# Which of two sets of PSUM banks a group takes, and when the down projection's combinations are issued

## The chip, the core and the metric

The program runs on one core of one Trainium2 chip. The metric is device microseconds of one execution. In this text PE is TensorE's matmul, PEld its weight load, DVE is VectorE, ACT is ScalarE, POOL is GpSimd, and SP is SyncE, which issues most of the loads.

## The reference, cut to what matters

The program is one encoder block on 256 rows of width 2048: a mixer of four parts, cross attention, and a gated feed-forward network (SwiGLU) of inner width 5632, each with a norm and a residual. Everything is float32. The change lies in the feed-forward network:

```python
def swiglu(h, w_gate_up, w_down):
    gate, up = jnp.split(h @ w_gate_up, 2, axis=-1)
    return (jax.nn.silu(gate) * up) @ w_down
...
        x = x + swiglu(rms_norm(x, norm_g[l, 2]), w_gate_up[l], w_down[l])
    return rms_norm(x, final_norm_g)
```

## The kernel before, in words

**Matmuls.** A float32 product is made of three matmuls of 128 x 128 by 128 x 512: high part of the activations times high part of the weights, high times low, low times high (`part`, L433 to L435). The 256 rows are two blocks of 128, so that one 128 x 512 block of weights gives six matmuls. The weights come as slabs of 1 MB (16 blocks of 128 x 128) from one array `W`, in the order of their use, into three buffers `raw`. A slab is split in halves: ACT casts the high part `wh` (L135, L159) and DVE subtracts it to get the low part `wl` (L136, L160). The buffers of the halves come free when PE has used them.

**Slabs of two kinds.** In the feed-forward network most work goes by `paired_rows` (L452). A plan tells what each slab is. `N` is a plain slab: four inner indices k, two row blocks, 24 matmuls. `S` is a slab for one pair of inner indices by a scheme of seven products in place of eight (Strassen's, in Winograd's form): its weights are summed on DVE first (L157, and for the gate and up projection partly in the loads, tile `two`), its activations are combined on DVE (`combine`, L438: eight adds and subtracts on 128 or 256 columns, plus two casts on ACT), and it has 21 matmuls. Four of the seven products go into sums of their own, called 1, 5, 6 and 7 in the code; the others go into the plain results a0, a1, b0, b1 (a and b are the two column blocks of 512, 0 and 1 the two row blocks).

**Banks.** PSUM has eight banks of 128 x 512. Four belong to a pool that `gbank` draws from (tiles `pg`) and four to a pool of `bank` (tiles `pm`). Within `paired_rows`, `put` (L465) draws a bank when a name is first used: a0, a1, b0, b1 from `gbank`, the sums from `bank`. A pool gives its four banks in turn, and the first matmul into a bank waits until the last reader of the tile that held it is done.

**Gate and up projection** (`gate_up`, L1033). Eleven groups of 512 + 512 columns. The first runs without sums; the ten others follow the plan `GROUP = "NNSNSNSN"`, 5 x 24 + 3 x 21 = 183 matmuls each. After the last S of a group `mixed` (L1050) reads the sums: a copy of q1 on ACT (L1053), then DVE adds with q6, q7 and q5. `gated` (L1059) adds a0 and a1 to the gate and applies Silu on ACT, and after the last N `upped` (L1065) adds b0 and b1, multiplies, transposes (L543) and stores the hidden rows to memory by POOL (L545).

**Down projection** (`down`, L1124). Two passes of 22 slabs, by the plans

```python
PASSES = "NNNNNNSNNSNNSNNSNNSNNN", "NNSNSNSNSNSNSNNNNNNNNN"
```

The hidden rows come back turned by POOL (L550) and are split by ACT and DVE (L291, L283). The combinations of the five S of the first pass and the sixth of the second come from a generator, `combined` (L1137).

**What sets the order.** The program is written in one order, with generators (`Background`) stepped in between when an estimate of PE's progress says so (`poll`) or when something must be ready (`drain` steps one until it ends). From that text a scheduler makes an order for each engine, and it may move an instruction when it takes its bank or operand to be late. Where one group with sums follows another (j = 2 to 10 in `gate_up`), it lets the group before the change begin with ten matmuls into a0, and the first into a1 is the eleventh.

Of the kernel before, what the change touches and what calls it, by code (L numbers as in the profile page):

```python
# [27 lines left out]
DFF = 5632  # L28
# [16 lines left out]
GROUP = "NNSNSNSN"  # L45
# [159 lines left out]
class Background:  # L205
# [17 lines left out]
    def first(self, g):  # L223

        self.q.sort(key=lambda e: e[0] is not g)
# [29 lines left out]
class Block:  # L255
# [193 lines left out]
        for i, x in enumerate((v, w)):  # L449
            self.split2(z[:, i * R:i * R + R], z[:, 512 + i * R:512 + i * R + R], x)  # L450

    def paired_rows(self, w, cols, slots, sums, plan, mixed, first, ready=None, late=0, before=None):  # L452

        st, s, nk = self.st, len(sums), len(slots)
        rest = [k for k in range(nk) if not any(k in ks for ks, _ in sums)]
        steps = [(c, k) for c in range(2) for k in rest]  # L460
        todo, q = iter(sums), {}
        count = {"a0": len(rest) + s, "a1": len(rest) + s, "b0": len(rest) + s, "b1": len(rest)}
        left, total = {}, 0

        def put(name, hi, lo, wh, wl):  # L465
            if name not in q:
                q[name] = self.gbank() if name in count else self.bank()
                left[name] = count.get(name, s)
            new = left[name] == count.get(name, s)
            left[name] -= 1  # L470
            self.part(q[name][:, :], hi, lo, wh, wl, new, left[name] == 0)

        form = lambda t, r: (t[:, r * P:(r + 1) * P], t[:, R + r * P:R + (r + 1) * P])
        n = done = 0
        for i, kind in enumerate(plan):
            if before:
                before(i)
            if kind == "S":
                ks, z = next(todo)
                a = [form(slots[ks[0]], 0), form(slots[ks[1]], 0), form(slots[ks[1]], 1)]  # L480
                x1, s2, s3, x4 = ((z[:, i * P:i * P + P], z[:, 512 + i * P:512 + i * P + P]) for i in range(4))
                t = (("5", x1), ("7", s3))
                pairs = iter((("1", a[0]), ("b0", x4), ("a0", a[1]), *(t if st.n // 16 in SUMMED else t[::-1]), ("a1", a[2]), ("6", s2)))
                for parts in st.take_sums(w, ks, cols):
                    for wh, wl in parts:
                        name, (hi, lo) = next(pairs)
                        put(name, hi, lo, wh, wl)
                        self.bg.poll()
                done += 1
                if done == s:  # L490
                    mixed(*(q[i] for i in "1567"))
            else:
                for c, k in steps[n:n + 4]:
                    if ready:
                        ready(k)
                    wh, wl = st.take(w, k, cols[c], 4)
                    for r in range(2):
                        put("ab"[c] + str(r), *form(slots[k], r), wh, wl)
                        self.bg.poll()
                n += 4  # L500
            if first and done == s and n >= len(rest):
                first(q["a0"], q["a1"])
                first = None
        assert n == len(steps) - late and done == s
        return [q["b0"], q["b1"]], rest[len(rest) - late:]
# [527 lines left out]
    def gate_up(self, gp, f, z):  # L1033

        nc = self.nc
        box, g, stored = {}, {}, []

        def gate(ps):
            for r in range(2):
                g[r] = gp.tile([P, 512], F32, name=f"g{r}", tag=f"g{r}")  # L1040
                nc.scalar.activation(g[r], ps[r], AF.Silu, scale=box["col"][:, r:r + 1])

        def up(j, ps, h=None):
            h = h or [gp.tile([P, 512], F32, name="h", tag="h", bufs=2) for _ in range(2)]
            for r in range(2):
                self.stt(h[r], ps[r], box["col"][:, r:r + 1], g[r], ALU.mult, ALU.mult)
                self.store_turned(self.ff, 4 * j, r, g[r], h[r])
            stored.append(self.bg.now)

        def mixed(q1, q5, q6, q7):  # L1050

            g[0], g[1], h[0], h[1] = (gp.tile([P, 512], F32, name=n, tag=n, bufs=b) for n, b in (("g0", 1), ("g1", 1), ("h", 2), ("h", 2)))
            nc.scalar.copy(g[0], q1)  # L1053
            self.tt(h[0], g[0], q6, ALU.add)
            self.tt(g[1], h[0], q7, ALU.add)
            self.tt(h[0], q5, h[0], ALU.subtract)
            self.tt(h[1], q5, g[1], ALU.subtract)

        def gated(*ps):  # L1059

            for r in range(2):
                self.tt(g[r], g[r], ps[r], ALU.add)
                nc.scalar.activation(g[r], g[r], AF.Silu, scale=box["col"][:, r:r + 1])

        def upped(j, ps):  # L1065

            for r in range(2):
                self.tt(h[r], h[r], ps[r], ALU.add)
            up(j, h, h)

        h = {}

        def fetch(k0, k1, ahead, pause, wait=0):

            m = {}
            for k in range(k0, k1 + ahead):
                if k < k1:
                    while len(stored) <= k // 4:
                        yield
                    m[k] = self.tmp()  # L1080
                    self.load_turned(m[k], self.ff, k)
                if k >= k0 + ahead:
                    while wait and self.bg.now < stored[(k - ahead) // 4] + wait:
                        yield
                    mark = self.mark()
                    self.split(f[k - ahead], m.pop(k - ahead))
                    self.keep_place(mark)
                    self.have = k - ahead + 1
                    yield pause

        def norm():

            mark = self.mark()
            nc.scalar.activation(self.mg[:, 0:1], self.mg[:, 0:1], AF.Silu)
            self.keep_place(mark)
            yield 2.0
            self.row_norm(1, box)
            yield

        arrival = lambda: gp.tile([P, R], F32, name="ar", tag="ar", bufs=4)  # L1100
        last = self.bg.add(self.arrive(self.xf[1], 3, arrival, self.put3, FAR), go=True)
        col = self.bg.add(norm())

        def combined():
            for ks, z in sums:
                yield 3.0
                yield from self.combine(z, *(self.h3[k] for k in ks))

        sums = [((2 * i, 2 * i + 1), z[i]) for i in range(GROUP.count("S"))]
        comb = self.bg.add(combined())  # L1110
        ps = self.gemm_rows("w_gate_up", [0, DFF], self.h3,
                            parts=[(range(8), [0]), (range(8, 12), [0]), (range(12), [1]), (range(12, 16), [0]), (range(12, 16), [1])],
                            before=lambda n: n in (1, 3) and self.bg.drain(self.late if n == 1 else last))
        self.bg.drain(col)
        gate(ps[0])
        up(0, ps[1])
        early = self.bg.add(fetch(0, FT - 22, 3, 2.0, 15))
        self.bg.drain(comb)
        for j in range(1, DFF // 512):
            upped(j, self.paired_rows("w_gate_up", [j * 512, DFF + j * 512], self.h3, sums, GROUP, mixed, gated)[0])  # L1120
        self.bg.drain(early)
        self.fetch = self.bg.add(fetch(FT - 22, FT, 6, SOON))

    def down(self, f, sp):  # L1124
# [9 lines left out]
        sums = [((2 * i, 2 * i + 1), x) for i, x in enumerate(z)]  # L1134
        made, split = [], []
# [31 lines left out]
        def done(c, *ps):  # L1167

            for r, p in enumerate(ps):
                x = self.half(c, r)  # L1170
                self.tt(x, x, p, ALU.add)
                squares(x, c, r)
# [6 lines left out]
        for i, plan in enumerate(PASSES):  # L1179
            n = plan.count("S")  # L1180
            g = self.bg.add(combined(n))
            late = (0, LATE)[i]
            plan = plan[:22 - late // 4]

            def before(j):
                if j == plan.index("S"):
                    self.bg.drain(g)
                if late and j == len(plan) - 2:
                    st.extra = None

            ps, rest = self.paired_rows("w_down", [2 * i * 512, (2 * i + 1) * 512], f, sums[:n], plan,
                                        lambda *q: mixed(2 * i, *q), lambda *q: done(2 * i, *q), ready, late, before)
            if i == 0:
                done(1, *ps)
        return ss, ps, rest, split
# [681 lines left out]
```

## Time and profile before

| | |
|---|---|
| median of 3 runs | 1444.63 us (1441.95 to 1446.84) |
| the profiled execution's own time | 1443.87 us |
| its span | 1442.1 us |
| matmul and weight load pairs on PE | 6601 |
| gate and up projection, j = 2 to 10 | about 819 to 1198 us of the span |
| down projection, first pass | about 1198 to 1318 us |

The span runs from the program's first to its last instruction on the engines. Matmuls are pipelined: a 128 x 512 matmul shows a length of 0.39 us and the next one begins 0.227 us after it, so that PE is busy without a gap while it is fed. An idle stretch before an instruction stands in brackets behind it, with what ended it. A wait is put down to the instruction that came last.

### The profile page before, as it was taken

To read this page: it belongs to the slowest core of one execution; us is meant where nothing else is said; L and a number is where in the kernel's file an instruction comes from. 1 tells how busy PE (TensorE), PEld (TensorE's weight loads), DVE (VectorE), ACT (ScalarE), POOL (GpSimd) and SP (SyncE) were. 2 spreads that over 40 slices of the span, in tenths; PEclk is the share of its full clock that TensorE was granted. 3 is DMA by queue.
4 is the path that set the end of the run, shared out by engine and by line. 5 is a ranking of instruction groups with operands and counts; after the bars stand their busy time and mean duration, and the time that the engine had idled before them with its cause. 6 is when DMAs were issued, how large, how long until landed. Compare 5 with 4: busy or idle time off the path is not lost.

```text
span 1442.1 us, 18599 instructions
## 1 busy us (share of the span) xinstructions
PE 1426.6 (99%) x6601; PEld 1183.1 (82%) x6601; DVE 1125.6 (78%) x1681; ACT 807.5 (56%) x1160; POOL 234.8 (16%) x306
## 2 busy tenths in 40 slices
PE   9999999999999999999999999999999999999997
PEld 8888888888888888888888888888888878788886
DVE  6667868777977666676676888889888889978884
ACT  7556655446655555555555555555555556555553
POOL 0000100012312233530421112112211103000000
PEclk9999999999999999999999999999999999999999
DMA  9886564456667788864976998989999877645563
GB/s 357 296 287 242 204 216 152 170 180 220 204 204 222 240 260 266 270 207 153 295 238 206 281 304 272 284 266 279 280 290 294 263 229 266 200 180 193 216 221 130
DMA packets 73039, 343.80 MB, mean 238 GB/s; under 512 B 10958, under 2 KB 12655, under 8 KB 45169
## 3 DMA queue, kind: packets, MB, share of 16 engines
q1 hardware_dynamic: 54848, 288.98, 57.4%
q0 software_dynamic: 17664, 52.97, 15.4%
q8 instruction: 52, 0.85, 0.2%
q10 hardware_dynamic: 432, 0.66, 0.1%
q14 instruction: 43, 0.34, 0.1%
HBM read 322.12 MB, written 20.45 MB: 238 GB/s over the span
## 4 chain that ended last, share of the span: by engine, by line
PE 93%; DVE 3%; DMA 2%; ACT 1%; issue 0%; ACTq 0%; DVEq 0%
PE pg L433 25%; PE pg L435 25%; PE pg L434 25%; PE pg L381 4%; DMA raw<-in_W 2%; PE pm L434 2%; PE pm L433 2%; PE pm L435 2%; PE pg L382 2%; DVE wl L136 1%; PE pm L1330 1%; PE pm L1008 1%; ACT wh L135 1%; PE pm L979 1%; DVE wl L160 0%
## 5 line engine op out<-in xcount | busy, mean ns | idle before, releaser
L136 DVE TENSOR_TENSOR wl<-raw,wh 128x1024 fp32r<-128x1024 f32 (+1 forms) x421 | 504.6, 1212 | 175.4 <-ACT wh L135 172.1
L135 ACT CAST wh<-raw 128x1024 fp32r<-128x1024 f32 (+1 forms) x421 | 433.2, 1043 | 303.1 <-PE pg L435 216.0
L433 PE MATMUL pg<-wh,act 128*128 128x512 f32 (+1 forms) x1454 | 567.9, 391 | 3.4 <-DVE g L283 3.3
L434 PE MATMUL pg<-wl,act 128*128 128x512 f32 (+1 forms) x1454 | 566.5, 390 | 2.1 <-DVE wl L160 1.1
L435 PE MATMUL pg<-wh,act 128*128 128x512 f32 (+1 forms) x1454 | 566.1, 390 | 0.5 <-DVE act L283 0.5
L433 PEld LDWEIGHTS pg<-wh,act 128*128 128x128 f32 x1454 | 273.3, 188 | 63.5 <-DVE g L283 5.9
L434 PEld LDWEIGHTS pg<-wl,act 128*128 128x128 f32 x1454 | 273.3, 188 | 59.1 <-DVE wl L136 2.3
L435 PEld LDWEIGHTS pg<-wh,act 128*128 128x128 f32 x1454 | 273.1, 188 | 58.2 <-DVE act L283 1.1
L159 ACT CAST wh<-raw 128x1024 fp32r<-128x1024 f32 (+1 forms) x134 | 122.4, 918 | 143.9 <-PE pg L435 82.9
L160 DVE TENSOR_TENSOR wl<-raw,wh 128x1024 fp32r<-128x1024 f32 (+1 forms) x134 | 139.0, 1058 | 63.4 <-ACT wh L159 63.1
L381 PE MATMUL pg<-act,wh 128*128 128x512 f32 x256 | 90.5, 395 | 0.0
L382 PE MATMUL pg<-act,wl 128*128 128x256 f32 x256 | 71.8, 280 | 0.0
L102 POOL DMA_DIRECT2D two<-in_W x30 | 26.6, 886 | 243.6 <-DMA two<-in_W 138.3
L159 ACT CAST wh<-two 128x1024 fp32r<-128x1024 f32 x30 | 31.5, 1051 | 52.6 <-PE pg L435 43.6
L381 PEld LDWEIGHTS pg<-act,wh 128*128 128x128 f32 x256 | 48.1, 188 | 10.5
L157 DVE TENSOR_TENSOR raw<-raw 128x512 f32<-128x512 f32 x74 | 51.1, 690 | 1.7
L550 POOL DMA_DIRECT2D tmp<-hidden x44 | 38.8, 889 | 58.3 <-issue 22.1
L382 PEld LDWEIGHTS pg<-act,wl 128*128 128x128 f32 x256 | 48.2, 188 | 0.2
L160 DVE TENSOR_TENSOR wl<-two,wh 128x1024 fp32r<-128x1024 f32 x30 | 36.7, 1223 | 7.2 <-ACT wh L159 7.1
L545 POOL DMA_DIRECT2D hidden<-g x22 | 17.2, 788 | 143.3 <-DVE g L543 143.3
L434 PE MATMUL pg<-wl,f 128*128 128x512 f32 x94 | 36.6, 389 | 0.0
L435 PE MATMUL pg<-wh,f 128*128 128x512 f32 x94 | 36.6, 389 | 0.0
(362 smaller groups left out, 1678.0 us busy)
## 6 DMA issues: line engine op xcount, KB each, us to landing
raw<-in_W SPq DMA_DIRECT2D x216, 1024.0 KB, 5.6
raw<-in_W SPq DMA_DIRECT2D x30, 768.0 KB, 6.7
two<-in_W SPq DMA_DIRECT2D x60, 256.0 KB, 5.0
two<-in_W POOLq DMA_DIRECT2D x30, 512.0 KB, 9.2
raw<-in_W SPq DMA_DIRECT2D x11, 512.0 KB, 7.2
hidden<-g POOLq DMA_DIRECT2D x22, 256.0 KB, 3.7
tmp<-hidden POOLq DMA_DIRECT2D x44, 128.0 KB, 5.5
features<-tmp POOLq DMA_DIRECT2D x32, 128.0 KB, 5.0
```

Source lines behind the costliest of these rows:

```text
L102: nc.gpsimd.dma_start(t, W[:, 512:1536], accum_op=ALU.add)
L135: nc.scalar.copy(wh[:, a:b], r[:, a:b])
L136: nc.vector.tensor_tensor(out=wl[:, a:b], in0=r[:, a:b], in1=wh[:, a:b].bitcast(F32), op=ALU.subtract)
L157: nc.vector.tensor_tensor(out=out, in0=a, in1=b, op=ALU.add)
L159: nc.scalar.copy(wh, src)
L160: nc.vector.tensor_tensor(out=wl, in0=src, in1=wh.bitcast(F32), op=ALU.subtract)
L381: self.nc.tensor.matmul(p[:, :], wh, slot[:, :], start=start, stop=False)
L382: self.nc.tensor.matmul(p[:, 0:R], wl, slot[:, 0:R], start=False, stop=stop)
L433: self.nc.tensor.matmul(p, hi, wh, start=start, stop=False)
L434: self.nc.tensor.matmul(p, hi, wl, start=False, stop=False)
L435: self.nc.tensor.matmul(p, lo, wh, start=False, stop=stop)
L550: self.nc.gpsimd.dma_start(t.rearrange("p (g t) -> p g t", t=32), src)
```

## The change

Two things. In `paired_rows` a new argument `swap` lets the two pools trade places: with it a0, a1, b0 and b1 come from `bank` and the sums from `gbank`. It is set for every second group of the gate and up projection (j = 2, 4, 6, 8, 10) and for the second pass of the down projection. Also the four sums are drawn together when the first of them is used, in the order 1, 6, 7, 5. In the down projection the drain of the generator at the first S is gone: at each S it is stepped only until as many combinations are made as that S needs, and otherwise it goes on as a background generator.

```diff
-    def paired_rows(self, w, cols, slots, sums, plan, mixed, first, ready=None, late=0, before=None):
+    def paired_rows(self, w, cols, slots, sums, plan, mixed, first, ready=None, late=0, before=None, swap=False):
...
         def put(name, hi, lo, wh, wl):
             if name not in q:
-                q[name] = self.gbank() if name in count else self.bank()
-                left[name] = count.get(name, s)
+                for x in [name] if name in count else "1675":
+                    q[x] = (self.bank if (name in count) == swap else self.gbank)()
+                    left[x] = count.get(x, s)
...
         for j in range(1, DFF // 512):
-            upped(j, self.paired_rows("w_gate_up", [j * 512, DFF + j * 512], self.h3, sums, GROUP, mixed, gated)[0])
+            upped(j, self.paired_rows("w_gate_up", [j * 512, DFF + j * 512], self.h3, sums, GROUP, mixed, gated, swap=j % 2 == 0)[0])
...
             def before(j):
-                if j == plan.index("S"):
-                    self.bg.drain(g)
+                while plan[j] == "S" and len(made) <= plan[:j].count("S"):
+                    self.bg.step(next(e for e in self.bg.q if e[0] is g))
...
             ps, rest = self.paired_rows("w_down", [2 * i * 512, (2 * i + 1) * 512], f, sums[:n], plan,
-                                        lambda *q: mixed(2 * i, *q), lambda *q: done(2 * i, *q), ready, late, before)
+                                        lambda *q: mixed(2 * i, *q), lambda *q: done(2 * i, *q), ready, late, before, i == 1)
```

## The prediction

> **What bounds the kernel now.** I read the page first: how much of the span TensorE (PE) works.
>
> ```profile
> span 1442.1 us, 18599 instructions
> PE 1426.6 (99%) x6601; PEld 1183.1 (82%) x6601; DVE 1125.6 (78%) x1681; ACT 807.5 (56%) x1160; POOL 234.8 (16%) x306
> ```
>
> The profiled execution took 1443.87 us, 1.8 over its span. All sums below start from it; it is 0.76 under the median of the three runs, 1444.63 (1441.95 to 1446.84). PE idles 15.5 us in all, so a change that leaves the matmuls as they are can win only where PE stops. The waits of PE say at whom it stops (us in total, times, longest):
>
> ```profile
> PE pg L433 <- DVE g L283: 3.3, 5, 1.0
> PE pg L434 <- DVE wl L160: 1.1, 1, 1.1
> PE pm L587 <- DVE eps L588: 1.1, 1, 1.1
> PE pg L434 <- DVE wl L136: 1.0, 1, 1.0
> PE pg L435 <- DVE act L283: 0.5, 1, 0.5
> ```
>
> Apart from L587, at the program's start, these are the two places that the diff touches: five stops where a group of the gate and up projection begins, three in the first pass of the down projection. First one of the five, in PE's timeline (start, length, line):
>
> ```profile
> 944.81 0.39 PE L433 MATMUL pg<-wh,act 128*128 128x512 f32 x1
> ...
> 946.85 0.39 PE L433 MATMUL pg<-wh,act 128*128 128x512 f32 x1
> 947.99 0.50 PE L433 MATMUL pg<-wh,act 128*128 128x512 f32 x1 [0.75 <-DVE g L283]
> 948.32 0.39 PE L434 MATMUL pg<-wl,act 128*128 128x512 f32 x1
> ```
>
> Ten matmuls start between 944.81 and 946.85, so one takes 2.04 / 9 = 0.227. Across the stop the starts lie 1.14 apart (0.91 too many), and the next two 0.33 (0.11 too many): 0.75 of idle time cost 1.02, so a stop costs its idle time plus 0.27. VectorE (DVE) in the same stretch:
>
> ```profile
> 940.78 0.68 DVE L283 TENSOR_TENSOR h<-g,pm 128x512 f32<-128x512 f32 x1
> ...
> 946.11 1.23 DVE L136 TENSOR_TENSOR wl<-raw,wh 128x1024 fp32r<-128x1024 f32 x1 [1.12 <-ACT wh L135]
> 947.25 0.68 DVE L283 TENSOR_TENSOR g<-g,pg 128x512 f32<-128x512 f32 x1
> 947.85 1.28 DVE L283 TENSOR_TENSOR h<-h,pg 128x512 f32<-128x512 f32 x2
> ...
> 951.59 1.19 DVE L136 TENSOR_TENSOR wl<-raw,wh 128x1024 fp32r<-128x1024 f32 x1
> ```
>
> The add of 947.25 (`gated`, second row block) empties the bank that the eleventh matmul wants. It stands behind the weight split of 946.11, which waited 1.12 for a cast on ScalarE (ACT). What the cast waits for shows in the chain of waits of the group before (start, length, what), whose next links are the cast and the split:
>
> ```profile
> 894.83 7.57 DMA raw<-in_W
> ```
>
> A 1 MB load of 7.57, the cast, the split of 1.23, then the add: the bank comes late because its add queues behind a late load, not because DVE is short of time.
>
> **The change, part by part.** *The banks.* With the sets trading places at every group, a0 takes the bank that held q1 of the group before, and a1 that of q6 ("1675" is the order in which `mixed` reads them). The order of the changed program confirms it: a1's first matmul stands fourth instead of eleventh and waits for the add that reads q6. q1 is copied here:
>
> ```profile
> 935.80 0.58 ACT L1053 COPY g<-pm 128x512 f32<-128x512 f32 x1
> ```
>
> That ends at 936.38, 8.4 before the group's first matmul (944.81). The add of q6 (940.78) ends at 941.46, 4.0 before the fourth matmul (944.81 + 3 x 0.227 = 945.49). Both release far ahead of need, so the five stops go: 3.3 + 5 x 0.27 = **4.65**. The other way round, the four sums now take the banks of a0, a1, b0, b1. The last reader of those is the pair of adds at 947.85, done by 949.13; the first sum's matmul stands 48 matmuls into the group, at 944.81 + 48 x 0.227 = 955.7. Cover 6.6, cost nothing. No instruction is added and no shape changes; ACT, POOL and SP keep their order in this stage.
>
> What is late next: the split of 951.59, second half of the group's second slab, done at 952.78. Its matmul stands 37 in: 944.81 + 37 x 0.227 = 953.21. So 0.43 is left, and 0.18 at the longest stop (1.0, 0.25 more than this one). I cost it at nothing; its cover is thin, and a load longer by more than that turns into a stop there.
>
> *The combinations.* The three stops of the down projection, and DVE before them:
>
> ```profile
> 1234.13 0.39 PE L433 MATMUL pg<-wh,act 128*128 128x512 f32 x1
> 1235.65 0.50 PE L434 MATMUL pg<-wl,act 128*128 128x512 f32 x1 [1.12 <-DVE wl L160]
> ...
> 1238.06 0.51 PE L434 MATMUL pg<-wl,act 128*128 128x512 f32 x1 [0.97 <-DVE wl L136]
> ...
> 1242.04 0.73 PE L435 MATMUL pg<-wh,act 128*128 128x512 f32 x2 [0.51 <-DVE act L283]
> ```
>
> ```profile
> 1229.81 1.22 DVE L160 TENSOR_TENSOR wl<-raw,wh 128x1024 fp32r<-128x1024 f32 x1
> 1230.95 0.49 DVE L283 TENSOR_TENSOR tmp<-tmp 128x128 f32<-128x128 f32 x2
> ...
> 1234.04 0.41 DVE L283 TENSOR_TENSOR tmp<-f 128x256 f32<-128x256 f32 x1
> 1234.38 1.22 DVE L160 TENSOR_TENSOR wl<-raw,wh 128x1024 fp32r<-128x1024 f32 x1
> ...
> 1241.57 0.42 DVE L283 TENSOR_TENSOR act<-tmp,act 128x256 fp32r<-128x256 f32 x1
> ```
>
> Their cost is 1.12 + 0.97 + 0.51 + 3 x 0.27 = **3.41**. The drain at the first S pushes the third, fourth and fifth combination through DVE at once, thirteen of their instructions between two weight splits of the first sums' slab, though that slab reads only the first combination, made long before. In the changed order three of the thirteen stay between these splits (one of 256 columns, two of 128, at most 0.91 by the rows of 1230.95 and 1234.04). So the second split starts at about 1231.9 instead of 1234.38 and is done at 1233.1. Its cast must be there:
>
> ```profile
> 1230.52 1.05 ACT L159 CAST wh<-raw 128x1024 fp32r<-128x1024 f32 x1 [1.21 <-PE pg L435]
> ...
> 1240.95 1.05 ACT L159 CAST wh<-raw 128x1024 fp32r<-128x1024 f32 x1 [1.45 <-DMA raw<-in_W]
> ```
>
> It is (1231.57). PE asked at 1234.13 + 0.23 = 1234.36, with two matmuls pulled ahead that the changed order puts back, so it will ask at 1233.9: 0.8 is left. The next weight split, for which the second stop waited, stands one instruction (0.42) behind: done at 1233.1 + 0.42 + 1.22 = 1234.7, asked for six matmuls after 1233.9, at 1235.3: 0.6 left. For the third stop, between 1230.95 and 1241.57 DVE now does four weight splits of 1.22, and the other 5.7 are combinations and small waits. Four combination instructions stay, 1.4 at most, so the split of the fetched row is 4.3 earlier, while PE comes 3.4 earlier: 0.9 left. The rest of the fourth and fifth combination, under 16 instructions of 0.28 to 0.42 or some 5 us, goes into the next two slabs of sums; DVE has 16.4 idle in that stage (second row):
>
> ```profile
> 819.00:1198.00 379.00, 375.59 (x1651) 309.05 (x1650) 324.91 (x385) 213.78 (x249) 60.11 (x70) 1.00 0.90 276
> 1198.00:1318.00 120.00, 117.40 (x516) 96.22 (x515) 103.61 (x158) 66.28 (x93) 12.98 (x15) 1.00 0.63 214
> ```
>
> (PE, PEld, DVE, ACT, POOL busy, granted clock, DMA share, GB/s.) The POOL queue keeps its order; two late fetches of hidden rows get free buffers earlier. The second pass and the final norm only change bank names.
>
> The sum: 1443.87 - 4.65 - 3.41 = 1435.8; from the median, 1436.6. I say **1436.0**. The unknown cost, new stops behind thin covers, lies between nothing and the gain of the place where it arises (4.65 or 3.41); I take nothing, since every step worked out above keeps cover. Below nothing: a stop too short for the list still costs its 0.27, and I allow for one, 0.3.
>
> **The rivals.** *A, the weight split takes the bank's place.* The 0.43 and 0.18 of cover go, and PE waits for the second slab's second half instead. For it: the DMA share of 0.90 from 819 to 1198, and a load that lasted 9.25:
>
> ```profile
> 1139.55 9.25 DMA raw<-in_W
> ```
>
> Against it: both halves keep their place on DVE, and no bytes are added. If the first part is given back: 1443.87 - 3.41 = **1440.5**.
>
> *B, fetched rows queue behind a weight split that waits for its load.* In the changed order the splits of the fetched rows of the second slab after the first sums stand behind the next sums' first weight split. That one's cast (1240.95) waited for a load that could begin at 1234.38 + 1.22 = 1235.6, so 5.3. It would now begin at 1233.1, the cast start at 1238.4, and cast, split and row split (1.05 + 1.22 + 0.42) end at 1241.1. PE asks 32 matmuls after the first sums end (1233.9 + 5 x 0.227 = 1235.04), at 1242.3. A load of 7.57 makes 1.1 of stop, one of 9.25 makes 2.7 + 0.27. So the second part nearly goes: 1443.87 - 4.65 = **1439.2**. [...]
>
> *C, slower: the loads give way.* Place: the load before each of ten group starts. PE ahead asks for loads sooner, at a share of 0.90; if they lengthen beyond 7.57 + 0.43 = 8.0, every us is PE's. At a mean of 8.8 the whole gain is gone (10 x 0.8); at 9.25 everywhere, 1443.87 - 8.06 + 10 x 1.25 = **1448.3**. Against it: the bytes are the same and the rate rises by 8 in 1444.
>
> *D, nothing happens*, because the stops come from the loads and reappear whole: **1443.9**. Against it: the release times above.
>
> *E, the stops cost clock too*, and more than their length comes back. The rows by stage give a granted clock of 1.00 with the stops in them; rounding hides at most 0.005 of 499 us, 2.5: **1433.3**. [...]
>
> **How the numbers follow.** Forecast 0.59, A 0.12, B 0.14, C 0.06, D 0.07, E 0.02. A run of this kernel cannot be told from no change within 0.3%, 4.3 us: the line is 1440.3. Forecast, B and E lie under it (0.75), A and D within (0.19), C above (0.06). The range takes the forecast with the runs' spread below their median (2.7) and the short stop (0.3), 1433.0, and reaches over B and A to 1441.5; C and D stay out.
>
> **What would show it.** Right: PE's waits have no row with g L283, nor wl and act rows near 1235; PE idles about 6 us less; a1's first matmul follows a0's third by 0.227; groups start 183 x 0.227 = 41.5 apart. A shows as PE waits for wl L136 some 8 us into a group, B as PE waits for act L283 near 1240, C as a median of the 1 MB loads well above this one's, D as PE idle of the same length under other names. Wrong at the root would be stops that remain on g or on q6's add.

## The result, and the profile after

The changed kernel takes **1437.51 us** (median of 8 runs, 1435.85 to 1440.93) against 1445.74 for the kernel before beside it (8 runs, 1441.34 to 1450.35): a ratio of 0.9948, interval 0.9928 to 0.9967. A later set, run beside some of the experiments below, gives 1437.96 (6 runs, 1436.61 to 1440.51) against 1444.10 (17 runs): 0.9957, 0.9943 to 0.9971. That is 6 to 8 us faster; 1436.0 was predicted, a gain of 8.6 from the median of before.

The page of the changed kernel's profiled execution (own time 1439.07), its first two lines:

```profile
span 1436.3 us, 18592 instructions
PE 1425.4 (99%) x6601; PEld 1182.9 (82%) x6601; DVE 1125.1 (78%) x1681; ACT 806.0 (56%) x1160; POOL 234.7 (16%) x306
```

PE's matmuls are the same 6601, and PE idles 10.9 us where it idled 15.5. Whom PE waits for in the changed kernel (us in total, times, longest; lines after L467 stand one lower in the file than before):

```profile
PE pm L588 <- DVE eps L589: 1.1, 1, 1.1
PE pg L434 <- DVE wl L136: 0.9, 3, 0.5
PE pm L434 <- DVE wl L160: 0.3, 1, 0.3
```

Every row that the prediction wanted to remove is gone: g L283, and the three near 1235. Two rows are new. The 0.9 of L136 lies at 7.7, 9.5 and 13.6 us, in the first loads of the program, where the diff touches nothing. Still, three profiles of the kernel before idle by 0.0 to 0.2 between 7 and 14 us, and three of the changed one by 0.5 to 1.2; a variant of the changed kernel (`raw4_after_b`, below) has 0.2 again. Whether that is chance was not settled, and the prediction has no term for it. The 0.3 of L160 comes from the change. PE's timeline at that place (start, length, line):

```profile
918.56 0.39 PE L433 MATMUL pm<-wh,act 128*128 128x512 f32 x1
919.24 0.50 PE L434 MATMUL pm<-wl,act 128*128 128x512 f32 x1 [0.29 <-DVE wl L160]
919.58 0.39 PE L435 MATMUL pm<-wh,act 128*128 128x512 f32 x1
```

The starts are 0.68 and 0.34 apart, 0.57 more than two steps of 0.227. It is the last weight split of a group's first S slab. Two shorter ones, at 835.04 and 876.99 (0.14 and 0.07 of idle time), stand at the same slab of the groups j = 2 and 3. Together they idle 0.50 and cost 0.50 + 3 x 0.27 = 1.3. With them the profiles' difference is accounted for: 8.06 of old stops, less 1.3, less the 1.1 by which PE is later after the first loads, makes 5.7; the spans differ by 5.8.

Where the new stop comes from shows on ACT and DVE of the changed kernel, first at the group's second slab:

```profile
904.61 1.05 ACT L135 CAST wh<-raw 128x1024 fp32r<-128x1024 f32 x1 [4.57 <-DMA raw<-in_W]
```

```profile
905.69 1.23 DVE L136 TENSOR_TENSOR wl<-raw,wh 128x1024 fp32r<-128x1024 f32 x1 [1.28 <-ACT wh L135]
...
916.09 0.68 DVE L157 TENSOR_TENSOR raw<-raw 128x512 f32<-128x512 f32 x1
917.96 1.23 DVE L160 TENSOR_TENSOR wl<-raw,wh 128x1024 fp32r<-128x1024 f32 x1 [1.19 <-ACT wh L159]
```

It ends the same kind of chain as the old stop did: the cast waits for a 1 MB load, which was issued at 896.61, and the first weight split of that slab waits for the cast. From there DVE does everything of that slab and the next in order behind the late data, with no idle stretch but the 1.2 in which ACT casts the last half, so the lateness runs on to the end of the S slab, 15 us after the group's start. (The view that follows the chain back from its end names another load here, of 8.90 from 902.05. That one is for the fourth slab; DVE is busy without a gap when it lands, so it delays nothing.)

The stage of the nine groups j = 2 to 10, in the row of busy times of the changed kernel (PE, PEld, DVE, ACT, POOL, clock, DMA share, GB/s):

```profile
819.00:1198.00 379.00, 378.50 (x1666) 311.88 (x1665) 329.22 (x392) 214.25 (x250) 60.11 (x70) 1.00 0.90 278
```

PE is busy for 378.50 of 379 us, where it was for 375.59, with 15 matmuls more in the same time.

### The profile page after: what moved, and what is told of

It reads as the page before. It is cut to its first block, busy times and chain, and to the rows that moved or that the text cites. A ratio compares the mean times of both kernels' runs of the same rounds, so it can differ in the third digit from the quotient of the medians.

```text
span 1436.3 us, 18592 instructions
## 1 busy us (share of the span) xinstructions
PE 1425.4 (99%) x6601; PEld 1182.9 (82%) x6601; DVE 1125.1 (78%) x1681; ACT 806.0 (56%) x1160; POOL 234.7 (16%) x306
## 4 chain that ended last, share of the span: by engine, by line
PE 96%; DVE 1%; DMA 1%; ACT 1%; issue 0%; SPq 0%; ACTq 0%; DVEq 0%
PE pg L433 21%; PE pg L434 21%; PE pg L435 21%; PE pm L434 7%; PE pm L435 7%; PE pm L433 7%; PE pg L381 4%; PE pg L382 2%; DMA raw<-in_W 1%; PE pm L1331 1%; PE pm L1009 1%; PE pm L980 1%; DVE wl L160 1%; DVE wl L136 0%; PE pm L1740 0%; ACT wh L159 0%
## 5 line engine op out<-in xcount | busy, mean ns | idle before, releaser
L136 DVE TENSOR_TENSOR wl<-raw,wh 128x1024 fp32r<-128x1024 f32 (+1 forms) x421 | 504.4, 1212 | 177.4 <-ACT wh L135 174.4
L433 PE MATMUL pg<-wh,act 128*128 128x512 f32 (+1 forms) x1187 | 463.8, 391 | 0.0
L434 PE MATMUL pg<-wl,act 128*128 128x512 f32 (+1 forms) x1187 | 462.4, 390 | 1.0 <-DVE wl L136 0.9
L435 PE MATMUL pg<-wh,act 128*128 128x512 f32 (+1 forms) x1187 | 462.2, 389 | 0.0
L434 PEld LDWEIGHTS pg<-wl,act 128*128 128x128 f32 x1187 | 223.1, 188 | 48.0 <-DVE wl L136 2.3
L433 PEld LDWEIGHTS pg<-wh,act 128*128 128x128 f32 x1187 | 222.9, 188 | 47.8 <-issue 1.5
L435 PEld LDWEIGHTS pg<-wh,act 128*128 128x128 f32 x1187 | 222.9, 188 | 46.7 <-DVE act L283 0.2
L160 DVE TENSOR_TENSOR wl<-raw,wh 128x1024 fp32r<-128x1024 f32 (+1 forms) x134 | 138.9, 1058 | 58.8 <-ACT wh L159 58.7
L434 PE MATMUL pm<-wl,act 128*128 128x512 f32 x305 | 119.1, 390 | 0.4 <-DVE wl L160 0.3
L433 PE MATMUL pm<-wh,act 128*128 128x512 f32 x305 | 118.7, 389 | 0.0
L435 PE MATMUL pm<-wh,act 128*128 128x512 f32 x305 | 118.7, 389 | 0.0
L434 PEld LDWEIGHTS pm<-wl,act 128*128 128x128 f32 x305 | 57.2, 188 | 13.5 <-DVE wl L160 1.3
L433 PEld LDWEIGHTS pm<-wh,act 128*128 128x128 f32 x305 | 57.2, 188 | 11.9
L435 PEld LDWEIGHTS pm<-wh,act 128*128 128x128 f32 x305 | 57.2, 188 | 11.7
L102 POOL DMA_DIRECT2D two<-in_W x30 | 26.6, 885 | 243.5 <-DMA two<-in_W 153.7
```

The source lines that it names most:

```text
L102: nc.gpsimd.dma_start(t, W[:, 512:1536], accum_op=ALU.add)
L136: nc.vector.tensor_tensor(out=wl[:, a:b], in0=r[:, a:b], in1=wh[:, a:b].bitcast(F32), op=ALU.subtract)
L160: nc.vector.tensor_tensor(out=wl, in0=src, in1=wh.bitcast(F32), op=ALU.subtract)
L433: self.nc.tensor.matmul(p, hi, wh, start=start, stop=False)
L434: self.nc.tensor.matmul(p, hi, wl, start=False, stop=False)
L435: self.nc.tensor.matmul(p, lo, wh, start=False, stop=stop)
```

## The experiments

**Each part alone.** `banks_only` is the change without its last part:

```diff
-                while plan[j] == "S" and len(made) <= plan[:j].count("S"):
-                    self.bg.step(next(e for e in self.bg.q if e[0] is g))
+                if j == plan.index("S"):
+                    self.bg.drain(g)
```

and `comb_only` is the kernel before with the reverse of this edit, its banks untouched.

> The changed kernel with the old drain: the bank sets trade places, and the combinations of the first pass are still drained at the first S. My theory (two independent parts): the five stops on the gate's adds (g, L283) are gone and the three stops near 1235 us of the span stay, 2.6 us of idle time, 3.4 us of cost; against before the median falls by 4.65 less about 1.2 of new short stops, so by 3.5 to 4.7 us, ratio 0.9968 to 0.9976. Rival 1 (the stops come from the loads and reappear under another name): no gain, ratio 1.000, with PE waits for weight splits of about 3 us in the gate and up stage. Rival 2 (the banks alone carry the whole gain, because PE's lead changes what collides in the down projection): ratio 0.995 and no stop near 1235.

> The kernel before with only the new stepping of the combinations in the down projection; the banks stay as before. My theory: the five stops on g (L283) stay, 3.3 us idle; the three stops near 1235 us (L160 1.1, L136 1.0, act L283 0.5) are gone; the median falls by 3.4 us, ratio 0.9976. Rival 1 (the fetched rows' splits queue behind a weight split that waits for its load): a stop on act L283 near 1240 us of 0.5 to 2.7 us remains and the gain is 1 to 2.5 us. Rival 2 (the drain is hidden anyway, and only banks count): ratio 1.000.

Against a kernel before of 1443.19 beside them, `banks_only` takes 1440.86 (ratio 0.9990, 0.9978 to 1.0001) and `comb_only` 1440.26 (0.9977, 0.9966 to 0.9988): 2.3 and 2.9 us by the medians, 1.4 and 3.3 by the ratios. `comb_only` came out as expected; `banks_only` gained less than the 3.5 to 4.7 expected of it, and its interval alone doesn't tell it from no gain. PE's waits with the banks alone:

```profile
PE pg L434 <- DVE wl L136: 1.7, 3, 1.0
PE pg L434 <- DVE wl L160: 1.1, 1, 1.1
...
PE pg L435 <- DVE act L283: 0.5, 1, 0.5
PE pm L434 <- DVE wl L160: 0.4, 1, 0.4
```

The bank stops are gone, the three near 1235 are as they were, and a new stop at the first S slab (at 835.12) is there too: it belongs to the trade of the banks. With the combinations alone, PE's waits are the other way round:

```profile
PE pg L433 <- DVE g L283: 2.8, 3, 2.1
PE pm L587 <- DVE eps L588: 1.1, 1, 1.1
PE pg L434 <- DVE wl L136: 0.5, 2, 0.2
PE pg L433 <- ACT wh L135: 0.4, 1, 0.4
```

Nothing is left near 1235. Each part removes its own stops, but the sum of the two gains, 5.2, was less than the 8.2 of the first comparison. So one question was open: do the parts help each other, or do the bank stops differ from run to run?

**A fourth load buffer.** If the bank is late because its add stands behind a late load, an earlier load must remove the bank stops with banks and drain untouched. The loads of the first and the third S slab of each group (768 KB) get a buffer of their own:

```diff
-        self.raw = self.rawp.tile([P, 2048], F32, name="raw", tag="raw")
+        if self.rawx and n // 16 in SUMMED and n // 16 % 4 == 2:
+            self.raw = self.rawx.tile([P, 1536], F32, name="raw", tag="raw")
+        else:
+            self.raw = self.rawp.tile([P, 2048], F32, name="raw", tag="raw")
```

(`rawx` is one buffer that lives through the gate and up projection.) `raw4_before` has it on the kernel before, `raw4_after` and, in the second set, `raw4_after_b` on the changed one.

> The kernel before, banks and drain as before, with a fourth load buffer in the gate and up stage for half of the S slabs (the third and the seventh slab of a group), so that the loads of the other slabs can start a slab earlier. It tells apart why the bank came late. My theory (the gate's add queues behind a weight split whose cast waits for a late load): with the loads early the five stops on g (L283) go although the banks do not trade places: PE waits for g under 0.5 us in total, median down by 3.5 to 5 us, ratio 0.9965 to 0.9976. Rival 1 (DVE is simply short of time at the group's end, so the bank is late whatever the load does): the stops stay, 2.5 to 3.3 us idle, ratio 0.999 to 1.000. Rival 2 (earlier loads collide with the accumulating loads and stores): stops stay or grow, ratio 1.000 to 1.002.

> The changed kernel with the same fourth load buffer. In the changed kernel's profile three short stops are left in the gate and up stage, where a group's first S slab waits for its last weight split (L160: 0.14, 0.07, 0.30 idle, 1.3 us of cost with 0.27 each). My theory (they are the end of the same late load, handed on through the cast, the adds and the weight sums): they go, and the median is 0.5 to 1.5 us under the changed kernel's, ratio to before 0.9937 to 0.9945. Rival (they come from DVE's own backlog after the group's end): they stay, ratio as the changed kernel's, 0.9948.

`raw4_before` takes 1439.59 (ratio 0.9971, 0.9956 to 0.9986). PE's waits in it (its lines stand three lower):

```profile
PE pg L437 <- DVE wl L163: 1.1, 1, 1.1
PE pm L590 <- DVE eps L591: 1.1, 1, 1.1
PE pg L437 <- DVE wl L139: 1.0, 1, 1.0
PE pg L438 <- DVE act L286: 0.5, 1, 0.5
```

All bank stops are gone with the banks as they were, and the three of the down projection stay. `raw4_after` takes 1436.28 (0.9951, 0.9938 to 0.9965; 0.9937 to 0.9945 was expected), with no stop in either stage, not even the short ones at L160: those too were the end of late loads, and not a lack of time on DVE. The runs close up: `raw4_before` stays within 1438.90 to 1440.55, `raw4_after` within 1435.09 to 1437.15, while the kernel before went from 1441.57 to 1453.65 beside them. And between these two, which no late load reaches, lies 3.31: the combinations' part by itself.

**The kernels themselves again.** In two later sets the kernel before was profiled twice more (`before_look_a` in the second set, `before_look_b` in the third), the changed one twice (`after_again` in the second, `after_look_b` in the third), and in the second set the banks alone and the buffer were timed beside them. The edits are those above.

> The kernel before, unchanged, profiled once more. Theory: the stops at the bank of a1 are the end of late loads, so their number and size change from execution to execution; the row of g L283 in PE's waits, 3.3 us over 5 stops in the first profile, should differ by 1 us or more, while the three stops of the first pass of the down projection, which come from the order on DVE, stay within 0.3 us each of 1.1, 1.0 and 0.5. Rival: the bank is late by a fixed order of work, and then the row is 3.3 again within 0.3 over the same five groups.

> The kernel before once more. Theory, that late loads come as they come: the groups whose first matmul into a1 stops are not the same as in either profile so far (j = 3, 4, 7, 8, 9 in the first, j = 1, 4 and 8 in the second), and their sum lies between 2.5 and 5.5 us; the three stops of the down projection are 1.1, 1.0 and 0.5 within 0.1, the last one gone where the first second is longer. Rival: the same groups as in one of the two.

PE's waits in `before_look_a` (1444.29), first rows:

```profile
PE pg L433 <- DVE g L283: 3.4, 3, 1.4
PE pg L434 <- DVE wl L136: 1.2, 2, 1.0
PE pg L434 <- DVE wl L160: 1.1, 1, 1.1
```

and in `before_look_b` (1442.0):

```profile
PE pg L433 <- DVE g L283: 1.3, 4, 0.4
PE pg L434 <- DVE wl L136: 1.1, 2, 1.0
PE pg L434 <- DVE wl L160: 1.1, 1, 1.1
```

The first has the same total as the profile before, against what was expected of it, but other groups: j = 2, 5 and 9, where the first profile has 4, 5, 8, 9 and 10 (the numbers in the second expectation are one too low). The second has j = 2, 4, 9 and 10 and less than half the total, less than expected. With `comb_only` (j = 2, 5 and 9), four executions of the same gate and up projection lose 3.3, 3.4, 1.3 and 2.8 of idle time to these stops, or with 0.27 for each 4.65, 4.2, 2.4 and 3.6: on average 3.7. It is not all chance: j = 9 stops in all four, j = 3, 6 and 7 in none. The kernel before is not one time but a spread, and the profile that the prediction priced lay at its upper end for this term.

> The changed kernel once more, beside two kernels on the same chip. Theory: 6 to 8 us under the kernel before on this chip (ratio 0.9945 to 0.9960), with zero to four stops below 0.5 us at the last weight split of the first slab with sums of a group, at other groups than 2, 3 and 4 as it happens. Rival, that these stops belong to groups 2, 3 and 4 by the order: the same three stops at the same places.

> The changed kernel once more. Theory: what is left of late loads shows as stops at L160 in the first slab with sums of a group, no more than 2 us in all, and no stop at g L283 in any group. Rival, that the trade only moved the late bank to where two profiles happened not to show it: a stop at g L283.

No stop at g L283 in either. `after_again` has two of the short ones, at j = 2 and 10 and neither idle by more than 0.08; `after_look_b` has one, at j = 2, and it is the last of PE's waits there:

```profile
PE pg L434 <- DVE wl L136: 0.5, 1, 0.5
PE pm L434 <- DVE wl L160: 0.3, 1, 0.3
```

So the trade of the banks gives back 1.3, 0.6 and 0.6 us (idle time and 0.27 for each) in three executions. Group j = 2 is among them each time, the others differ.

> The trade of the banks alone, with the drain as it was, once more beside the whole change. Theory, that the parts add up and the earlier run met small bank stops in the kernel before: the whole change is 3.4 us faster than this one (the down projection's three stops), within 1 us. Rival, that the parts help each other: the distance is over 4.5 us.

> The changed kernel with the fourth load buffer of 6 KB, once more beside the changed kernel itself. Theory: the buffer takes away the rest of late loads only, so it is 0.5 to 2 us faster than the changed kernel and its runs lie within 2.5 us of each other. Rival, that nothing is left to gain: the same time within 0.5 us.

`banks_only_b` takes 1441.23 (0.9983, 0.9973 to 0.9993). The changed kernel is 3.27 below it. That is the price of the combinations as the pair with the fourth buffer gave it (3.31), so the rival that the parts help each other, with a distance over 4.5, is out. Of the 6.1 measured in this set, 2.9 are left for the banks (1.0 to 3.9 by the interval). The 8.2 of the first comparison was 8 runs of a kernel that spreads over 9 us. `raw4_after_b` takes 1436.06 (1435.49 to 1436.97), ratio to before 0.9943 (0.9929 to 0.9957): 1.9 under the changed kernel in the same set. It is the fastest complete kernel of the study.

**Why the loads are late.** `noacc_before` and `noacc_after`, in the third set, leave out one line of `_load`, and with it one addend of the summed weights:

```diff
-            nc.gpsimd.dma_start(t, W[:, 512:1536], accum_op=ALU.add)
```

> The kernel before without the 512 KB load of each slab with sums that adds onto the tile two (30 of them, 9.1 us from issue to landing against 7.7 for the raw loads beside them); left out is thus one addend in the weights of those slabs, and 30 x 0.5 MB of transfer, nothing else. Theory, that the 1 MB loads before a group are late because they share the 16 DMA engines with that load: the stops at g L283 are gone or under 0.3 us each, the three of the down projection stay, 3 to 5 us faster than the kernel before on this chip. Rival, that the loads are late because the three buffers come free late: the stops at g L283 stay at 2 to 4 us in all, and the time stays within 1 us.

> The changed kernel with the same load left out (one addend in the weights of the slabs with sums). Theory: no stops in the gate and up projection, 3.4 us under the kernel before with the same load left out, that is, the down projection's part alone, and the trade of the banks is worth nothing. Rival, that the buffers make the loads late: the short stops at L160 stay, and the distance to the kernel before with the same load left out is 5 us or more.

`noacc_before` takes 1438.43 against 1443.40 (0.9968, 0.9956 to 0.9980), and PE is never idle in the stage of the groups, with three buffers and the banks as before:

```profile
819.00:1198.00 379.00, 379.00 (x1674) 313.83 (x1673) 329.65 (x392) 217.31 (x250) 37.53 (x46) 1.00 0.73 241
```

The loads of 1 MB in this stage, issue to landing (count, KB, median us), first in the kernel before, then without the accumulating load, then in the changed kernel:

```profile
raw<-in_W SPq DMA_DIRECT2D x46, 1024.0 KB, 6.9
```

```profile
raw<-in_W SPq DMA_DIRECT2D x46, 1024.0 KB, 5.5
```

```profile
raw<-in_W SPq DMA_DIRECT2D x47, 1024.0 KB, 7.4
```

Without the accumulating loads the 1 MB loads land sooner (5.5 for 6.9, at a DMA share of 0.73 for 0.90) and no bank is late: the accumulating loads beside them are one condition of the lateness. It is not the only one. In `raw4_before` the accumulating loads are there and the 1 MB loads take as long as before:

```profile
raw<-in_W SPq DMA_DIRECT2D x46, 1024.0 KB, 7.0
```

There no bank is late either: the edit lets the loads start sooner and does not shorten them (7.0 for 6.9). So it took both here, a long load and a buffer that comes free late, and either remedy was enough. Leaving out the line takes away the accumulation and 0.5 MB per slab together; these runs don't tell which of the two lengthens the others. `noacc_after` takes 1435.04 (0.9941, 0.9929 to 0.9954), without a stop in either stage. It lies 3.39 below `noacc_before`: where no load is late, the trade of the banks is worth nothing, and all of the difference is the combinations.

## Why the prediction was right, step by step

**Combinations, 3.41: right in size.** Three pairs of kernels that differ in this part alone measure it at 3.27, 3.31 and 3.39; beside the kernel before, where bank stops blur it, it was 2.9 (interval 1.7 to 4.9). The covers are there as worked out. DVE in the changed kernel:

```profile
1229.33 1.23 DVE L160 TENSOR_TENSOR wl<-raw,wh 128x1024 fp32r<-128x1024 f32 x1
...
1230.80 3.49 DVE L136 TENSOR_TENSOR wl<-raw,wh 128x1024 fp32r<-128x1024 f32 x3
```

and PE, where it asks for these two halves:

```profile
1231.63 0.39 PE L434 MATMUL pg<-wl,act 128*128 128x512 f32 x1
...
1232.99 0.39 PE L434 MATMUL pg<-wl,act 128*128 128x512 f32 x1
```

The first split is done at 1230.56 and asked for at 1231.63, so 1.1 is left (0.8 predicted); the second, the first of three joined in its row, at about 1232.0 and 1232.99, so 1.0 (0.6 predicted). Rival B does not show: no wait for act L283 near 1240.

**Banks, 4.65: right in mechanism, too large in size.** The releases came as far ahead as worked out: with the late load still there (DVE idles 1.28 before the weight split at 905.69, waiting for its cast), no a1 waits in any group of the changed kernel, and groups follow each other by 41.5 where no stop is left (946.48 to 987.96). But the two timed comparisons give 2.3 and 2.9 (1.4 and 2.5 by the ratios), with intervals that together reach from no gain to 3.9. Two things are off in the prediction. The term was read from one execution, and such stops vary: four profiles average 3.7. And the new short stops give back 0.6 to 1.3, where 0.3 was allowed.

**"What is late next", the step that failed.** The prediction looked at the second half of the group's second slab and found 0.43 and 0.18 of cover; that half held. The half that failed is the last of the S slab behind it, and the profile of before had what was needed. Its DVE and PE at j = 4, a group that had stopped:

```profile
915.85 1.23 DVE L160 TENSOR_TENSOR wl<-raw,wh 128x1024 fp32r<-128x1024 f32 x1 [1.19 <-ACT wh L159]
```

```profile
917.61 0.39 PE L433 MATMUL pg<-wh,act 128*128 128x512 f32 x1
917.83 0.39 PE L434 MATMUL pg<-wl,act 128*128 128x512 f32 x1
```

The split is done at 917.08, PE asks at 917.83: 0.75 of cover, after a stop that cost 0.58 + 0.27 = 0.85 at the bank. Take the stop away and PE asks 0.85 earlier, 0.1 too soon. At the same split j = 5 and 10 have 0.77 of cover, so their stops, which cost 1.02 and 1.26, would leave new ones of about 0.25 and 0.5. The old stop at the bank had been holding PE back for everything later in the group, so the cover behind it had to be compared with the whole cost of the stop, at each later half, and not with the nearest one alone.

**The rivals.** A, the weight split takes the bank's place, is what happened in part: at another split, and for 0.6 to 1.3 us of the 4.65 and not the whole. C, longer loads, is true in direction: 7.4 for 6.9 in that stage, but 8.0 was the point from which it would decide. D is out. E, that stops cost clock, got a chance of 0.02, since the rows by stage of before have a granted clock of 1.00 with the stops in them; two other profiles do show such a cost. In `comb_only` one bank stop of 2.07 is followed by matmuls 0.43 apart where 0.227 is usual. Its rows of busy times and, in the third last column, granted clock:

```profile
822.00:825.00 3.00, 0.93 (x5) 0.43 (x4) 1.93 (x3) 2.67 (x4) 0.00 (x0) 1.00 0.92 324
825.00:829.50 4.50, 4.50 (x13) 3.54 (x14) 4.50 (x7) 1.69 (x2) 1.17 (x2) 0.62 0.12 45
829.50:833.00 3.50, 3.50 (x17) 2.86 (x16) 2.91 (x5) 1.07 (x3) 0.40 (x1) 1.00 0.89 241
```

PE's 13 matmuls in 4.5 us should be 19 or 20; some 1.5 us are lost, beside the stop itself. From 826 to 828 the granted clock is 0.50, from 828 to 830 it is 0.64, and a mean of 0.62 over 4.5 us is what 3.4 us at half would give. In `before_look_a` the same follows the second of the down projection's stops:

```profile
1237.77 0.79 PE L434 MATMUL pg<-wl,act 128*128 128x512 f32 x1 [0.97 <-DVE wl L136]
1238.36 0.63 PE L435 MATMUL pg<-wh,act 128*128 128x512 f32 x1
```

There the granted clock is 0.50 from 1238 to 1240; it cost about 1.5, and the third stop (0.51 + 0.27) vanished in it. The six other profiles with these three stops keep a clock of 1.00 through them, from 1228 to 1246. So the clock fell after one idle stretch of 2.07, and after one of 1.13 and one of 0.97 within 3.6 us in one profile of seven; what decides it was not shown. E's cost thus came with some stops and not with others. It may be part of why the kernel before spreads over more us than its stops alone explain; that was not measured.

**Two remarks on the text ahead.** The pools don't give their banks in turn: in the built programs a pool hands out the bank that was released first. For the same reason drawing the four sums together as "1675" does nothing: a program built with the sums drawn one by one, each at its first use, is the same instruction by instruction, addresses and waits included (it was built, but not run).

What stays open is why the first comparison showed 8.2 and the second 6.1. Their intervals overlap (0.9928 to 0.9967, 0.9943 to 0.9971), and the runs of the kernel before spread enough for it, but which loads are late in a run was not settled.

## What to carry to other kernels

When a stop is removed, subtract its whole cost from the cover of every later need of the same late data until some engine's idle time breaks the chain; here the nearest one held and one 7 us later did not. The stops that end a load's chain differed from run to run (3.3, 3.4, 1.3 and 2.8 us of idle time in four executions), so that their price needed several profiles, while the stops made by the order on an engine (1.1, 1.0 and 0.4 to 0.5 in six profiles) could be priced from one. And a pair of kernels in which the disturbing cause is removed from both measures a small part of a change better than many runs beside the noisy original: 3.31 and 3.39 here, where the plain comparison gave 2.9 with an interval 3.2 us wide.

## What the runs showed of the hardware

The accumulating loads took more of the DMA engines here than their share of the bytes. Leaving them out (`noacc_before`, 819 to 1198) lowers the stage's rate from 276 to 241 GB/s, an eighth, and the DMA share from 0.90 to 0.73, a fifth: 35 GB/s for 0.17 of the engines, where the rest moves 241 for 0.73, so that a byte of them takes about 1.6 times the time of another, as an estimate that leaves the other traffic as it was. The rows by queue bear that out: the queue of the accumulating loads goes from 26.6% of the engines for 21.86 MB to 8.0% for 8.26 MB, the queue of the 1 MB loads only from 62.6% to 64.6%. How much of the price is accumulation and how much that queue is not shown: the other loads and stores on it also cost 1.0% per MB, against 0.8% on the queue of the 1 MB loads.

The granted clock fell to 0.50 after a single stop of 2.07 us (`comb_only`, 826 to 828) and after stops of 1.13 and 0.97 close together (`before_look_a`, 1238 to 1240). In both the rows of 2 us around the fall come to some 3.4 us at half, as an estimate (0.50 and 0.64; 0.92, 0.50 and 0.73). Six other profiles with the latter two stops keep 1.00 through them, so it happened in some executions and not in others.
